# Moving the norm of the per-layer embedding e into the MLP, and rewriting the first stage, in a one-core decoder layer

## The chip, the core and the metric

The kernel runs on one core of a Trainium2 chip. The metric is the device time of one execution in microseconds (us). In the text PE is the matmul engine, DVE the vector engine, ACT the scalar engine, POOL the GpSimd engine, and SP the engine whose queue issues all the DMA transfers spoken of here. A line such as L1191 is a line of the kernel before; PEclk is the granted clock of PE as a share of full speed.

## The reference

One decoder layer over 2048 tokens of width 1024 in fp32. Two groups of token mixers share one input projection; their outputs go through one output projection; then comes an MLP with a squared ReLU, and last an embedding e, normed and gated, is added.

```python
hn = rms_norm(h, pre_mix_norm)
proj = hn @ w_in                    # q, k, v, z, a, b (DeltaNet); f, i, q, g (HGRN2)
g_dec = -exp(gdn_a_log) * softplus(a + gdn_dt_bias);  beta = sigmoid(b)
o_a = gated_head_norm(gated_delta_rule_chunked(l2norm(silu(conv(q))), l2norm(silu(conv(k))),
                                               silu(conv(v)), g_dec, beta), gdn_norm, z)
o_b = gated_head_norm(hgrn2_chunked(...), hgrn_norm, g)
h = h + rms_norm(concat(o_a, o_b) @ w_out, post_mix_norm)
y = square(relu(rms_norm(h, pre_mlp_norm) @ w_mlp_up)) @ w_mlp_down
h = h + rms_norm(y, post_mlp_norm)
e = rms_norm(p @ w_ple_proj, ple_norm)
h = h + e * sigmoid(h @ w_ple_gate)
```

## The kernel before

The tokens are worked on in four quarters q of 512, and a tile holds 128 channels by 512 tokens. Every fp32 product is made of three matmuls: each operand is split into a hi part (an ACT copy to fp32r) and a lo part, called its rest (a DVE subtract), and hi·hi, hi·lo and lo·hi are summed in PSUM. The function split does both steps (L169 on ACT, L170 on DVE). A weight passes from a raw tile to a split one in that way, and in the mixers also from there to a cache in DRAM.

The stages in order of PE's time:

- *Beginning.* e = p · w_ple_proj for q 0 and 1, 16 tiles (PE mme; ACT copies each to an SBUF tile, SP stores it to the DRAM tensor ed). The functions make, take and put issue the matmuls, the copy and the store of one tile. Between them x of q 0 is squared and normed (hl, nrm, ss, diag, ps_rsb), scaled (L458) and split into xt, and the projection ab (the rows for the decay and beta) goes into the bank mm_ab (L468).
- *Mixers.* 33 jobs for each quarter, each a block of 128 columns of w_in: 24 matmuls into a bank `mm` (L1191), and behind them the work of the heads as a list of steps. The banks come in turn from two PSUM pools, two banks of them in the pool pm. The quarter's first step is `decays`: it reads the bank mm_ab, makes softplus and sigmoid rows in the tile gb, scans them, and stores them (gd). gf_g is the broadcast load of gd for a head. `y_qg` and `y_kg` are q and k of DeltaNet after the convolution; kk_g are their products in a chunk, u_g and the solve follow, xn_g is its result in transposed form and psp_g the matmul that reads it.
- *Fill.* The same embedding for q 2 and 3 (embed_tile) among the last steps of the mixers.
- *Out-projection.* `mmo` (L1260), with w_out's blocks made ready by ready_out; behind it the residual yo and the sums acc_h and acc_o of its squares, and the norm of h.
- *MLP in two halves (q 0 and 1, then q 2 and 3).* Up (bank u, 16 blocks g) and down (bank d), each as seven products in place of eight of 2 x 2 blocks. up_weights loads the four parts `a` of a block's weights and makes wu; `hidden` stores the five combinations of the block's results that down reads. In half 0 `summed` squares and adds up the tiles of o for q 2 and 3. `residual` with the name "y" adds the normed y to h and stores it to h2d.
- *Gate.* `mmg`, and e times the gate.

The norm of e is a sum of squares over 8 tiles for each quarter. In the beginning squares(accs...) makes them from the SBUF copies for q 0 and 1, behind the last xt; in the fill from the banks for q 2 and 3. norm_steps turns each sum into a row ple_r[q], through DRAM for the transposition.

What sets the order: PE's instructions and SP's stand as the program writes them. In the beginning ACT and DVE do too. Elsewhere a scheduler orders ACT, DVE and POOL by due times, tc.issue_after ties an instruction behind another one, and high_priority ranks it above the rest. A clock ticks every 8 matmuls; at(...) and later(...) spread the steps of a generator over such ticks, a yield between two of them. An engine runs its instructions in order, and so does SP: a DMA that waits for its source or for its target buffer holds all that stand behind it.

Of the kernel before, what the change touches and what calls it, by code (L numbers as in the profile page):

```python
# [47 lines left out]
MLP_STEPS = (1, 5) + tuple(range(7, 25, 2))  # L48
# [37 lines left out]
def trunk(ctx, tc, x, xT, pT, vecs, w_in, w_ab, gdn_a_log, gdn_dt_bias, w_out, w_up, w_down,  # L86
# [56 lines left out]
    def bounds():  # L143

        V.tensor_scalar(ple_w, cols[:, R_PLE : R_PLE + KD], 0.5, None, ALU.mult)
        V.tensor_tensor(lb, lg, lg, ALU.subtract)
        S.activation(lb, lb, AF.Exp)
        V.reciprocal(lb1, lb)
        V.tensor_tensor(lb, lb, lb1, ALU.mult)
        V.tensor_tensor(lb, lb, lb, ALU.subtract)  # L150
        V.tensor_scalar(ha, lb, -0.5, 0.5, ALU.mult, ALU.add)
        V.tensor_scalar(hna, ha, -1.0, None, ALU.mult)
        V.tensor_tensor(hb, lb, ha, ALU.add)
        S.activation(nexpa, dec[:, 0:1], AF.Exp)
        V.tensor_scalar(nexpa, nexpa, -1.0, None, ALU.mult)
# [158 lines left out]
    def embed_tile(q, d, w, pt, accs, pool, bufs):  # L314
# [10 lines left out]
    x_r, xts, accs = {}, {0: []}, {0: None, 1: None}  # L325
# [26 lines left out]
    def ready_out(j):  # L352
# [42 lines left out]

    staged, split_w = {}, {}
    with ExitStack() as ectx:
        es = ectx.enter_context(tc.tile_pool(name="es", bufs=1))
        ET = mybir.EngineType
        with tc.manual_schedule(engines={ET.SP, ET.Activation, ET.DVE}):  # L400
            praw = [es.tile([P, 2, QT], F32, name=f"praw{q}") for q in range(2)]
            xraw = es.tile([P, KD, QT], F32, name="xraw")
            sqe = [es.tile([P, QT], F32, name=f"sqe{i}") for i in range(8)]
# [26 lines left out]
            last_x = []  # L430
# [22 lines left out]
            def square_e(i):  # L453
                q, d = todo[i]
                accs[q] = squares(accs[q], es16[i], d, f"e{q}", V, lambda: (sqe + sqx[2:])[i - 2 if i > 4 else i - 1])

# [3 lines left out]
            def ready_x0(k):  # L460
                t = ra.tile([P, 2, QT], F32R, tag="ring", name=f"xt0_{k}")
                last_x[:] = [S.activation(t[:, 0], xraw[:, k], AF.Copy).ins,
                             V.tensor_tensor(t[:, 1], xraw[:, k], t[:, 0], ALU.subtract).ins]
# [29 lines left out]
            take(5)  # L493
            make(8)
            make(9)
# [23 lines left out]
            make(12)  # L519
            for c in range(NC):  # L520
                PE.matmul(rsb[:, blk(c)], one, diag[:, c], start=True, stop=True)
            take(8)
            split_w[1] = staged.pop(1)()
            take(9)
            put(0, 1, 2)
            staged[2] = stage("0_0_0", w_in[0])
            put(3, 4, 5, 6)
# [3 lines left out]
            later_makes = {0: 13, 1: 14, 3: 15}  # L531
            gone = 10
            for k in range(KD):
# [7 lines left out]
                if k in later_makes:  # L541
                    make(later_makes[k])
                if k == 2:
                    put(7, 8, 9)
                    staged[3] = stage("8_0_0", w_in[8])
            while gone < 16:
                take(gone)
                gone += 1
            put(*range(10, 16))
        with tc.issue_after(last_x[0]), tc.issue_after(last_x[1]):  # L550
            bounds()
            for i in range(2 * KD):
                square_e(i)


    with mixers as mctx:
# [51 lines left out]
        def decays(ps, q):  # L608

            gb = mt(f"gb_{q}", "gb", 1, (36, QT))  # L610
            sp = m2.tile([4, QT], F32, tag="tmp", name=f"sp_{q}")
            se = m2.tile([4, QT], F32, tag="th", name=f"se_{q}")
            S.activation(sp, ps[0:4, :], AF.Identity, bias=dec[:, 1:2])
            V.memset(gb, 0.0)
            S.activation(gb[32:36, :], ps[32:36, :], AF.Tanh, scale=0.5)  # L615
            V.tensor_scalar(gb[32:36, :], gb[32:36, :], 0.5, 0.5, ALU.mult, ALU.add)
            V.scalar_tensor_tensor(se, sp, -1.0, sp, ALU.mult, ALU.max)
            S.activation(se, se, AF.Exp, scale=-1.0)
            S.activation(se, se, AF.Ln, bias=1.0)
            V.scalar_tensor_tensor(sp, sp, 0.0, se, ALU.max, ALU.add)  # L620
            V.tensor_scalar(sp, sp, nexpa, None, ALU.mult)
            tied = ExitStack()
            if q:
                yield
                tied.enter_context(tc.issue_after(turns[-1]))
            for c in range(NC):
                V.tensor_tensor_scan(gb[0:4, blk(c)], one[0:4, :], sp[:, blk(c)], 0.0, ALU.mult, ALU.add)
            tied.close()
            gd = dr.tile([4, QT], F32, name=f"gd{q}")
            decay[q] = [gd, None]  # L630
            yield
            nc.sync.dma_start(gd, gb[0:4, :])
# [537 lines left out]
        for q in range(2):  # L1170
            at(0, norm_steps(accs[q], 1.0 / D, EPS, f"e{q}", partial(ple_r.__setitem__, q)),
               [12 + 6 * q + i for i in (0, 2, 4, 5, 6)])
        with tc.manual_schedule(engines={mybir.EngineType.SP}):
            assert [w[0] for w in works[:4]] == ["ab0", "4_0_0", "0_0_0", "8_0_0"]
            for j, (name, key, src, q, h, then, g, b) in enumerate(works):
                split_work(j + 2)
                if j:
                    stage_work(j + 3)
                keep_work(j)
                ps = bank(f"mm_{name}") if j else ps_ab  # L1180
# [5 lines left out]
                for s in range(SPT):  # L1186
# [5 lines left out]
                    if s == SPT - 1 and h is None:  # L1192
                        at(clock[0], decays(ps, q) if q else urgent(decays(ps, q)), (0, 2.5, 3, 5) if q else (0, 2, 6))
# [9 lines left out]
            accs, store = {q: None for q in qs}, None  # L1203
# [20 lines left out]
            while clock[0] <= last or len(held) < 2 or 1 in ready:  # L1224
                if fill:
                    q, d = fill.pop(0)
                    new = embed_tile(q, d, ple[d // 4], pts[q], accs, m2, 2)
# [3 lines left out]
                    if d == KD - 1:  # L1231
                        at(clock[0], norm_steps(accs[q], 1.0 / D, EPS, f"e{q}", partial(ple_r.__setitem__, q)),
                           [1 + i for i in (0, 2, 4, 5, 6)])
# [84 lines left out]
    def residual(q, y_of, rsb, skip, gain, dst, name, sums=None, late=late):  # L1318
# [3 lines left out]
        total, put = None, None  # L1322
        for d in range(KD):
            yield
            if put:
                nc.sync.dma_start(*put)
# [4 lines left out]
            put = dst[d], y  # L1331
# [3 lines left out]
        yield  # L1335
        nc.sync.dma_start(*put)
# [25 lines left out]
    def summed(q):  # L1362

        total, y = None, late(yod[q][0], f"ys{q}_0")
        for d in range(KD):
            yield
            nxt = late(yod[q][d + 1], f"ys{q}_{d + 1}") if d + 1 < KD else None
            total = squares(total, y, d, f"o{q}")
            y = nxt
        yield  # L1370
        yield from rstd_steps(total, 1.0 / D, EPS, f"o{q}", row_of(o_r, q), po, wait=True)
# [245 lines left out]
    def hidden(half, g, c):  # L1617

        n = f"{half}_{g}"
        keep_hidden(half, g, "22", c["22"])  # L1620
# [9 lines left out]
        yield  # L1630
        for k, t in (("1", t1), ("3", c["12"]), ("2", t2), ("4", t4)):
# [207 lines left out]
    for half in range(2):  # L1839
        for g in range(NG):  # L1840
# [10 lines left out]
            if half == 0 and g in (1, 3):  # L1851
                later(summed((g + 3) // 2), list(range(2, 20, 2)) + [20, 30, 33])
# [112 lines left out]
```

## Time and profile before

| | us |
|---|---|
| runs, median (lowest to highest) | 2725.13 (2724.48 to 2728.61) |
| profiled execution | 2726.73 |
| its span | 2724.9 |
| PE busy in the span | 2663.4 (98%) |
| DVE busy | 2046.8 (75%) |
| ACT busy | 1473.0 (54%) |

The profiled execution is one run of its own, with a granted clock of 0.995 on the mean. Busy shares are means over the whole span; the stages differ. PE's matmuls of 128x512 follow each other every 0.24 us in an undisturbed stretch (24 in 5.71 us), so a gap of a few us between two of them is a wait that the views name.

### The profile page before, as it was taken

What the parts mean: (1) busy time and instruction counts of PE and PEld (TensorE: products, weight loads), DVE (VectorE), ACT (ScalarE), POOL (GpSimd) and SP (SyncE); (2) the same over time, 40 slices, a digit from 0 to 9 for tenths busy, and PEclk for the clock granted to TensorE, in tenths of its full rate; (3) what the DMA queues carried; (4) which work ended last, traced back from release to release, by engine and by line L of the source; (5) the groups of instructions that cost most, each with busy time, mean ns of one, the idle gap of its engine ahead of it and who ended that gap; (6) DMA issues with size and microseconds to landing.
All of it is one profiled execution on the core that took longest, in us unless ns stands there. A gap on an engine that the chain in (4) does not pass through costs nothing. (4 is left out here: it accounts for less than half of the span.)

```text
span 2724.9 us, 38478 instructions
## 1 busy us (share of the span) xinstructions
PE 2663.4 (98%) x12761; PEld 2219.2 (81%) x12761; DVE 2046.8 (75%) x4243; ACT 1473.0 (54%) x2951; POOL 107.6 (4%) x118
## 2 busy tenths in 40 slices
PE   7899999999999999999999999999999999999999
PEld 5788788888888888778887788887888888887887
DVE  7788877787788777678779977858787765567775
ACT  6666555455546445676565556545555445465431
POOL 0000000000000000000000000001000000001000
PEclk9999999999999999999999999999999999999999
DMA  6867777666666665888456666657454356677663
GB/s 222 271 232 239 234 252 239 219 220 241 240 209 220 208 211 180 255 295 282 141 189 213 241 211 223 225 192 249 161 187 166 137 187 196 195 255 243 207 219 124
DMA packets 271223, 587.93 MB, mean 216 GB/s; under 512 B 55706, under 2 KB 60280, under 8 KB 253616
## 3 DMA queue, kind: packets, MB, share of 16 engines
q1 hardware_dynamic: 271024, 585.48, 64.2%
q8 instruction: 101, 1.65, 0.2%
q14 instruction: 98, 0.80, 0.1%
HBM read 421.58 MB, written 163.77 MB: 215 GB/s over the span
## 5 line engine op out<-in xcount | busy, mean ns | idle before, releaser
L1191 PE MATMUL mm<-xt,w 128*128 128x512 f32 x3072 | 785.3, 402 | 11.1 <-ACT gb L615 7.7
L1191 PEld LDWEIGHTS mm<-xt,w 128*128 128x128 f32 x3072 | 557.3, 189 | 116.2 <-ACT gb L615 8.1
L1260 PE MATMUL d<-db,da 128*128 128x512 f32 x2688 | 614.2, 391 | 3.9 <-DVE db L223 2.1
L1260 PE MATMUL u<-t,wu 128*128 128x512 f32 x2604 | 595.1, 391 | 4.8 <-ACT wu L169 3.7
L1260 PEld LDWEIGHTS d<-db,da 128*128 128x128 f32 x2688 | 505.5, 188 | 111.9 <-DVE db L223 4.5
L1260 PEld LDWEIGHTS u<-t,wu 128*128 128x128 f32 x2604 | 489.6, 188 | 109.3 <-ACT wu L169 4.8
L223 DVE TENSOR_TENSOR db<-db 128x512 fp32r<-128x512 f32 x224 | 160.8, 718 | 71.4 <-ACT db L222 70.0
L1645 DVE TENSOR_TENSOR u<-u,u 128x512 f32<-128x512 f32 x224 | 151.1, 685 | 59.8 <-PE u L1260 58.8
L222 ACT ACTIVATE db<-db 128x512 fp32r<-128x512 f32 x224 | 140.9, 629 | 81.3 <-DMA db<-hid 78.9
L1260 PE MATMUL mmg<-h2T,wg 128*128 128x512 f32 (+1 forms) x792 | 174.8, 383 | 0.0
L1260 PEld LDWEIGHTS mmg<-h2T,wg 128*128 128x128 f32 x792 | 145.7, 188 | 28.9
L1686 ACT ACTIVATE u<-u 128x512 f32<-128x512 f32 x128 | 80.8, 631 | 163.1 <-DVE u L1645 162.6
L1260 PE MATMUL mmo<-mixT,w_out 128*128 128x512 f32 x720 | 165.9, 392 | 2.5 <-DVE w_out L170 2.5
L1260 PEld LDWEIGHTS mmo<-mixT,w_out 128*128 128x128 f32 x720 | 136.3, 189 | 31.2 <-DVE w_out L170 2.9
L170 DVE TENSOR_TENSOR da<-da 128x512 fp32r<-128x512 f32 x128 | 94.1, 735 | 88.6 <-ACT da L169 88.2
L169 ACT ACTIVATE da<-da 128x512 fp32r<-128x512 f32 x128 | 80.5, 629 | 135.7 <-DMA da<-sumd 108.3
L169 ACT ACTIVATE wu<-a 128x512 fp32r<-128x512 f32 x124 | 74.0, 622 | 48.4 <-DMA a<-in_w_up_dram 45.7
L828 DVE TENSOR_TENSOR pr_g<-xs_g,sys_g 128x16 f32<-128x16 f32 (+14 forms) x240 | 94.2, 392 | 5.3
L233 POOL TENSOR_TENSOR acc_y<-acc_y,sq_y 128x512 f32<-128x512 f32 x28 | 38.6, 1378 | 1371.0 <-ACT sq_y L232 1371.0
L170 DVE TENSOR_TENSOR wu<-a,wu 128x512 fp32r<-128x512 f32 x124 | 85.2, 689 | 3.4 <-ACT wu L169 3.4
L1687 ACT ACTIVATE u<-u 128x512 f32<-128x512 f32 x128 | 80.6, 630 | 3.4
L170 DVE TENSOR_TENSOR da<-dr,da 128x512 fp32r<-128x512 f32 x96 | 66.4, 691 | 17.7 <-ACT da L169 15.4
(397 smaller groups left out, 3817.2 us busy)
## 6 DMA issues: line engine op xcount, KB each, us to landing
w<-cache_in SPq DMA_DIRECT2D x96, 1024.0 KB
db<-hid SPq DMA_DIRECT2D x224, 256.0 KB
cache_in<-w SPq DMA_DIRECT2D x32, 1024.0 KB
hid<-u SPq DMA_DIRECT2D x128, 256.0 KB
da<-sumd SPq DMA_DIRECT2D x128, 256.0 KB
a<-in_w_up_dram SPq DMA_DIRECT2D x124, 256.0 KB
hid<-ht SPq DMA_DIRECT2D x96, 256.0 KB
dr<-in_w_down_dram SPq DMA_DIRECT2D x96, 256.0 KB
```

The lines of the kernel that those rows point to most:

```text
L169: S.activation(t[:, 0], raw, AF.Copy)
L170: eng.tensor_tensor(t[:, 1], raw, t[:, 0], ALU.subtract)
L222: S.activation(t[:, 0], plain(t), AF.Copy)
L223: V.tensor_tensor(t[:, 1], plain(t), t[:, 0], ALU.subtract)
L233: eng.tensor_tensor(acc, acc, sq, ALU.add)
L828: V.tensor_tensor(pr[:, :, :, 0:i], xs[:, None, :, 0:i].broadcast_to([P, 2, GC, i]), sys[:, 0:i, i : i + 2].rearrange("p j two -> p two j" ...
L1191: PE.matmul(ps, *terms[i], start=i == 0, stop=i == nt - 1)
L1260: PE.matmul(ps, a, b, start=start, stop=stop)
L1645: V.tensor_tensor(c[new], c[old], ps, ALU.add)
L1686: S.activation(c[k], c[k], AF.Relu)
L1687: S.activation(c[k], c[k], AF.Square)
```

## The change

It has five parts.

1. *Norm of e.* The squares, the adds and the steps of its norm leave the beginning and the fill. In half 1 of the MLP `summed`, with source, name and target as arguments, loads the eight tiles of e of one quarter from ed, squares and adds them, and makes the row; one quarter each at the blocks g = 3, 6, 9 and 12 of the up projection.
2. *Beginning.* The order of makes, takes and puts is new; the rests of w_ab and of w_4_0_0 come earlier; w_0_0_0 is split in the loop over k; the load of 8_0_0 comes last. The rows of the decay for q 0 (decay_rows, the old body of decays) are made right behind ab, before the mixers begin. bounds() is left to the scheduler.
3. *Bank.* Job 2 takes its bank from the pool pp.
4. *w_out.* For the first blocks the rest is issued with high priority.
5. *Stores.* `hidden` issues the store of "22" one step later, beside the other four, except for the block (1, 0). `residual` with the name "y" stores a tile two steps behind its add, not one.

The core of the diff:

```diff
-MLP_STEPS = (1, 5) + tuple(range(7, 25, 2))
+MLP_STEPS = (1, 5) + tuple(range(7, 27, 2))
...
-        accs[q] = squares(accs[q], ps, d, f"e{q}")            # embed_tile
...
         if q < RAW:                                            # ready_out
-            split(w, V, raw)
+            S.activation(w[:, 0], raw, AF.Copy)
+            with tc.high_priority():
+                V.tensor_tensor(w[:, 1], raw, w[:, 0], ALU.subtract)
...
+    def decay_rows(ps, gb, sp, se, tied=ExitStack):
+        S.activation(sp, ps[0:4, :], AF.Identity, bias=dec[:, 1:2])
+        V.memset(gb[0:32, :], 0.0)
+        S.activation(gb[32:36, :], ps[32:36, :], AF.Tanh, scale=0.5)
...
             square_x(6)                                        # beginning
...
-            make(10)
+            make(9)
             w = split_w[0] = wp.tile([P, 2, KD, P], F32R, tag="whl", name="w_ab0")
             S.activation(w[:, 0], raw, AF.Copy)
+            V.tensor_tensor(w[:, 1], raw, w[:, 0], ALU.subtract)
...
-            V.tensor_tensor(w[:, 1], raw, w[:, 0], ALU.subtract)
+            make(10)
             make(11)
+            split_w[1] = staged.pop(1)()
+            take(8)
+            take(9)
             diag = sqx[1].rearrange("p (c j) -> p c j", c=NC)
...
-            split_w[1] = staged.pop(1)()
...
                 ready_x0(k)
-                if gone in sums:
-                    take(gone)
-                    gone += 1
+                if k in (0, 2, 4, 6):
+                    take(12 + k // 2)
+                elif k == 5:
+                    split_w[2] = wp.tile([P, 2, KD, P], F32R, tag="whl", name="w_0_0_0")
+                    S.activation(split_w[2][:, 0], staged[2], AF.Copy)
                 ab(k)
...
-                    staged[3] = stage("8_0_0", w_in[8])
...
+            put(*range(13, 16))
+            keep("ab", split_w[0])
+            staged[3] = stage("8_0_0", w_in[8])
+            for _ in decay_rows(ps_ab, first_gb, rest[:, 0], rest[:, 1]):
+                pass
-            bounds()
-            for i in range(2 * KD):
-                square_e(i)
+        bounds()
...
-                ps = bank(f"mm_{name}") if j else ps_ab
+                ps = bank(f"mm_{name}", pp if j == 2 else None) if j else ps_ab
...
-        total, put = None, None                                # residual
+        total, puts, lag = None, [], 2 if name == "y" else 1
...
-            if put:
-                nc.sync.dma_start(*put)
+            if len(puts) == lag:
+                nc.sync.dma_start(*puts.pop(0))
             if d + 1 < KD:
                 nxt, ynxt = late(skip(d + 1), f"x{name}{q}_{d + 1}"), y_of(d + 1)
...
-        keep_hidden(half, g, "22", c["22"])                    # hidden
+        if not STRASSEN_DOWN or (half, g) == (1, 0):
+            keep_hidden(half, g, "22", c["22"])
...
         yield
+        if (half, g) != (1, 0):
+            keep_hidden(half, g, "22", c["22"])
         for k, t in (("1", t1), ("3", c["12"]), ("2", t2), ("4", t4)):
...
+            if half == 1 and g in (3, 6, 9, 12):
+                q = g // 3 - 1
+                later(summed(q, ed[q], "e", ple_r), list(range(2, 26, 3)) + [26, 28, 32, 36])
```

How the order moves, at three places. A row gives the line, the operation, out<-in by name and number, and the shape; both kernels are listed apart, since lines and buffer numbers differ between them.

First ACT where the mixers begin. Before (sqx are squares of e here, sp and gb_657 the reading of the bank mm_ab):

```order
L232 ACTIVATE sqx_256<-e_272 128x512
L232 ACTIVATE sqx_257<-e_273 128x512
L232 ACTIVATE sqx_258<-e_274 128x512
L169 ACTIVATE w_0_0_652<-raw_0_0_468 128x1024
L169 ACTIVATE w_0_0_674<-raw_0_0_518 128x1024
L169 ACTIVATE hl_e_868<-acc_e_582 128x512
L613 ACTIVATE sp_658<-mm_ab_476,dec 4x512
L665 ACTIVATE acc_kg_0_707<-mm_0_0_681,cols 128x512
L666 ACTIVATE hist<-mm_0_0_681 128x3
L615 ACTIVATE gb_657<-mm_ab_476 4x512
```

After (xt_6 and xt_7 are the last tiles of the loop, sp_570 and gb_569 the reading of mm_ab):

```order
L456 ACTIVATE e_266<-mme_7_520 128x512
L167 ACTIVATE xt_7_555<-xraw 128x512
L397 ACTIVATE sp_570<-mm_ab_472,dec 4x512
L399 ACTIVATE gb_569<-mm_ab_472 4x512
L402 ACTIVATE sp_570<-sp_570 4x512
L404 ACT_TABLE_LOAD
L404 ACTIVATE sp_570<-sp_570 4x512
L675 ACTIVATE acc_kg_0_666<-mm_0_0_639,cols 128x512
L167 ACTIVATE w_0_0_632<-raw_0_0_567 128x1024
L676 ACTIVATE hist<-mm_0_0_639 128x3
```

The reading of mm_ab stood behind the squares of e, two weight copies and hl_e, with acc_kg of the next bank between its two halves; now it follows the last xt at once, and acc_kg comes behind it.

Second ACT around q of the first DeltaNet head (acc_qg is the start of its convolution, jk the sums of squares of k, cd, tail, e and kt read gf_g). Before:

```order
L665 ACTIVATE acc_qg_0_761<-mm_0_0_722,cols 128x512
L666 ACTIVATE hist<-mm_0_0_722 128x3
L678 ACTIVATE y_qg_0_768<-acc_qg_0_761 128x512
L765 ACTIVATE jk_g_0_0_816,ssk_g_0_805<-t_kg_0_810 128x128
L765 ACTIVATE jk_g_0_1_818,ssk_g_0_805<-t_kg_0_810 128x128
L765 ACTIVATE jk_g_0_2_820,ssk_g_0_805<-t_kg_0_810 128x128
L765 ACTIVATE jk_g_0_3_822,ssk_g_0_805<-t_kg_0_810 128x128
L169 ACTIVATE w_0_0_769<-raw_0_0_718 128x1024
L744 ACT_TABLE_LOAD
L744 ACTIVATE cd_g_0_785<-gf_g_0_731 128x4
L746 ACTIVATE tail_g_0_786<-tail_g_0_786 128x4
L750 ACTIVATE e_g_0_790<-e_g_0_790,gcol_758 128x128 x4
```

After:

```order
L167 ACTIVATE w_0_0_728<-raw_0_0_677 128x1024
L754 ACT_TABLE_LOAD
L754 ACTIVATE cd_g_0_744<-gf_g_0_690 128x4
L756 ACTIVATE tail_g_0_745<-tail_g_0_745 128x4
L760 ACTIVATE e_g_0_749<-e_g_0_749,gcol_717 128x128 x4
L761 ACTIVATE gf_g_0_690<-gf_g_0_690 128x512
L775 ACTIVATE jk_g_0_3_781,ssk_g_0_764<-t_kg_0_769 128x128
L777 ACTIVATE kt_g_0_774<-t_kg_0_769,tail_g_0_745 128x128 x4
L688 ACT_TABLE_LOAD
L688 ACTIVATE y_qg_0_727<-acc_qg_0_720 128x512
```

y_qg stood right behind the convolution and ahead of the work on gf_g; now it stands behind all of that and behind a table load of its own.

Third DVE in the out-projection (sq_h and sqo are squares of yo and of mmo; w_out_12909 is the block whose subtract starts at 1205.98 in the profile). Before:

```order
L1329 SCALAR_TENSOR_TENSOR yo_6_12594<-yo_6_12594,cols,r_o_12712 128x512
L233 TENSOR_TENSOR acc_h_12756<-acc_h_12756,sq_h_5_12857 128x512
L1330 TENSOR_TENSOR yo_6_12594<-yo_6_12594,xa_6_12766 128x512
L1329 SCALAR_TENSOR_TENSOR yo_7_12633<-yo_7_12633,cols,r_o_12712 128x512
L223 TENSOR_TENSOR mixT_6_12892<-mixT_6_12892 128x512
L1330 TENSOR_TENSOR yo_7_12633<-yo_7_12633,xa_6_12766 128x512
L233 TENSOR_TENSOR acc_h_12756<-acc_h_12756,sq_h_6_12875 128x512
L233 TENSOR_TENSOR acc_o_12679<-acc_o_12679,sqo_4_12906 128x512
L170 TENSOR_TENSOR w_out_12909<-raw_out_12851,w_out_12909 128x1024
L233 TENSOR_TENSOR acc_h_12756<-acc_h_12756,sq_h_7_12889 128x512
```

After:

```order
L231 TENSOR_TENSOR acc_o_12532<-acc_o_12532,sqo_3_12698 128x512
L231 TENSOR_TENSOR acc_h_12609<-acc_h_12609,sq_h_3_12667 128x512
L1336 TENSOR_TENSOR yo_4_12363<-yo_4_12363,xa_4_12593 128x512
L1335 SCALAR_TENSOR_TENSOR yo_5_12404<-yo_5_12404,cols,r_o_12565 128x512
L361 TENSOR_TENSOR w_out_12762<-raw_out_12704,w_out_12762 128x1024
L231 TENSOR_TENSOR acc_h_12609<-acc_h_12609,sq_h_4_12685 128x512
L1336 TENSOR_TENSOR yo_5_12404<-yo_5_12404,xa_4_12593 128x512
L1335 SCALAR_TENSOR_TENSOR yo_6_12447<-yo_6_12447,cols,r_o_12565 128x512
L1335 SCALAR_TENSOR_TENSOR yo_7_12486<-yo_7_12486,cols,r_o_12565 128x512
L231 TENSOR_TENSOR acc_h_12609<-acc_h_12609,sq_h_5_12710 128x512
```

Before, w_out_12909 stood among the sums of sq_h_6, sq_h_7 and sqo_4. The same block after, w_out_12762, stands ahead of the sum of sq_h_4 and of the last three steps on yo.

More of the change, by code (lines that the diff above doesn't have):

```diff
@@ L461, in ready_x0 @@
                 t = ra.tile([P, 2, QT], F32R, tag="ring", name=f"xt0_{k}")
-                last_x[:] = [S.activation(t[:, 0], xraw[:, k], AF.Copy).ins,
-                             V.tensor_tensor(t[:, 1], xraw[:, k], t[:, 0], ALU.subtract).ins]
+                split(t, V, xraw[:, k])
                 xts[0].append(t)
@@ L608, in decays @@
         def decays(ps, q):
[L610 to L622, printed above, removed]
-            if q:
-                yield
[L625 to L632, printed above, removed]
+            if q:
+                gb = mt(f"gb_{q}", "gb", 1, (36, QT))
+                rows = decay_rows(ps, gb, m2.tile([4, QT], F32, tag="tmp", name=f"sp_{q}"),
+                                  m2.tile([4, QT], F32, tag="th", name=f"se_{q}"),
+                                  lambda: tc.issue_after(turns[-1]))
+                for _ in range(3):
+                    next(rows)
+                yield
+                next(rows, None)
+                gd = dr.tile([4, QT], F32, name=f"gd{q}")
+                decay[q] = [gd, None]
+                yield
+                nc.sync.dma_start(gd, gb[0:4, :])
+            else:
+                gb, gd = first_gb, dr.tile([4, QT], F32, name="gd0")
+                decay[q] = [gd, None]
+                nc.sync.dma_start(gd, gb[0:4, :])
             yield
@@ L1334, in residual @@
             xk, y = nxt, ynxt
-        yield
-        nc.sync.dma_start(*put)
+        while puts:
+            yield
+            nc.sync.dma_start(*puts.pop(0))
         return total
```

91 lines of the change are left out of this document (46 added, 45 removed).

## The prediction

> **What bounds the kernel.** I read the page's engine shares first, then the waits of PE, then stretches of the span, then the timeline around each wait that the change touches. First the page:
>
> ```profile
> span 2724.9 us, 38478 instructions
> PE 2663.4 (98%) x12761; PEld 2219.2 (81%) x12761; DVE 2046.8 (75%) x4243; ACT 1473.0 (54%) x2951; POOL 107.6 (4%) x118
> ```
>
> PE is the bound. The change takes no matmul away: the eight that sum the squares of e for the norm are issued elsewhere. So it can only win what PE idles, 61.5 us (2724.9 less 2663.4), and what a cold clock costs behind an idle stretch. The waits of PE, as line waited for, total, times, longest:
>
> ```profile
> PE mm L1191 <- ACT gb L615: 7.7, 1, 7.7
> ...
> PE psp_g L852 <- DVE xn_g L847: 6.0, 2, 4.3
> ...
> PE u L1260 <- ACT wu L169: 3.7, 2, 2.8
> PE mmo L1260 <- DVE w_out L170: 2.5, 1, 2.5
> ...
> PE mm_ab L468 <- ACT xt L462: 1.9, 1, 1.9
> ...
> PE d L1260 <- ACT db L222: 1.7, 1, 1.7
> PE mm L1191 <- ACT zt_zg L704: 1.7, 1, 1.7
> PE nrm_h L1292 <- DVE hl_h L170: 1.2, 2, 0.6
> ...
> PE mme L196 <- ACT sq_e L232: 0.9, 1, 0.9
> PE mme L196 <- ACT acc_e L229: 0.9, 1, 0.9
> ```
>
> The waits are short ones in known places, and the edits aim at gb, xt, sq_e, acc_e, w_out, wu and db. Stretches of the span (length, busy time of each engine, granted clock, DMA share, GB/s):
>
> ```profile
> 30.00:40.00 10.00, 8.29 (x28) 6.49 (x29) 8.69 (x15) 6.03 (x11) 0.00 (x0) 0.83 1.00 360
> 50.00:60.00 10.00, 2.84 (x7) 2.27 (x8) 9.79 (x15) 8.01 (x13) 3.02 (x15) 0.67 0.47 156
> 1060.00:1120.00 60.00, 54.79 (x305) 45.35 (x304) 49.52 (x116) 42.27 (x92) 3.13 (x3) 1.00 0.55 171
> 1200.00:1210.00 10.00, 7.51 (x29) 5.78 (x28) 8.82 (x14) 7.37 (x13) 0.00 (x0) 0.86 0.61 219
> 1323.00:1383.00 60.00, 59.10 (x260) 48.41 (x259) 53.14 (x87) 41.53 (x73) 0.00 (x0) 1.00 0.63 207
> 1950.00:2240.00 290.00, 290.00 (x1281) 240.29 (x1281) 221.12 (x351) 148.03 (x246) 0.00 (x0) 1.00 0.49 169
> ```
>
> The reader sees three tight places (50 to 60, the fill at 1060 to 1120, 1200 to 1210) and one with no slack to win, the up projection of half 1 (1950 to 2240), where PE never stops.
>
> **The change, part by part.** *The beginning up to the ab projection.* DVE sets the pace of the loop that scales x and splits it into xt:
>
> ```profile
> 30.02 1.40 DVE L458 SCALAR_TENSOR_TENSOR xraw<-xraw,cols,ps_rsb 128x512 f32<-128x512 f32 x2
> 39.14 0.69 DVE L463 TENSOR_TENSOR xt<-xraw,xt 128x512 fp32r<-128x512 f32 x1 [1.27 <-ACT xt L462]
> 41.88 1.29 DVE L463 TENSOR_TENSOR xt<-xraw,xt 128x512 fp32r<-128x512 f32 x2 [1.39 <-ACT xt L462]
> ```
>
> Its two waits for ACT are 1.27 + 1.39 = 2.66 us; there ACT held a copy of e behind a matmul of PE. The new loop takes a copy of e only at k = 0, 2, 4, 6, from banks filled earlier. The subtract for w_4_0_0 (128x1024) stood between diag and the first scale and now stands ahead of diag, while ss is still being formed: another 1.2 us. Together 3.9; I take -3.5, and as ends -1.3 (one wait stays) and -4.5 (with the clock of 0.83 between 30 and 40 mended).
>
> *The wait for gb.* The third bank user waits until mm_ab's bank has been read, and that reading stands behind the squares of e:
>
> ```profile
> 47.67 3.22 ACT L232 ACTIVATE sqx<-e 128x512 f32<-128x512 f32 x6
> 49.78 3.30 DVE L233 TENSOR_TENSOR acc_e<-acc_e,sqx 128x512 f32<-128x512 f32 x5
> 56.00 0.48 DVE L614 MEMSET gb<- 36x512 f32 x1
> 56.52 0.59 ACT L615 ACTIVATE gb<-mm_ab 4x512 f32<-4x512 f32 x1 [0.32 <-DVE gb L614]
> 57.16 7.19 PE L1191 MATMUL mm<-xt,w 128*128 128x512 f32 x24 [7.65 <-ACT gb L615]
> 68.78 5.71 PE L1191 MATMUL mm<-xt,w 128*128 128x512 f32 x24
> ```
>
> With the squares and adds gone, gb read right after ab, and job 2's bank taken from the other pool, nothing of this is left: -7.65, and -1.48 for the 24 matmuls that ran cold (7.19 against 5.71): -9.1. Ends: -9.3, and -5 if job 3's weights, whose load now goes out last of the beginning, are the next to be late.
>
> *What is late next: y_qg.* The order of ACT now puts the table load, cd, tail, e, gf, kt and a second table load ahead of y_qg, which before stood ahead of them. The rows of before:
>
> ```profile
> 64.42 0.32 SPq L734 DMA_DIRECT2D gf_g<-gd  x1
> ...
> 68.12 0.63 ACT L678 ACTIVATE y_qg<-acc_qg 128x512 f32<-128x512 f32 x1 [2.98 <-DVE acc_qg L670]
> ...
> 71.42 1.28 ACT L744 ACT_TABLE_LOAD   x1
> 72.71 0.21 ACT L744 ACTIVATE cd_g<-gf_g 128x4 f32<-128x4 f32 x1
> ...
> 74.62 1.10 ACT L767 ACTIVATE kt_g<-t_kg,tail_g 128x128 f32<-128x128 f32 x4
> ...
> 74.33 0.38 PE L788 MATMUL kk_g<-y_kg 128*128 128x128 f32 x2
> ```
>
> The first use of the loaded gf, from the view of its tile:
>
> ```profile
> L745 DVE TENSOR_TENSOR tail_g<-gf_g,gcol x16: 155/157/171, 72.1 to 999.4; 128x4 f32<-128x4 f32 x16
> ```
>
> The first job ended at 57.16 - 7.65 = 49.5, so the mixers began at 49.5 - 5.7 = 43.8; after, at 40.3, with job 2 from 46.0. kk stood 74.33 - 57.16 = 17.2 us behind job 2's start, 15.7 without the cold 1.5, so kk is due at 61.7, and t_kg (done at 68.78, 5.55 ahead of kk) at 56.15. ACT finished kt at 75.72, 6.9 us behind t_kg: after, at 63.1. One more table load (1.28) and y_qg (0.63) end at 65.0, so kk waits 3.3 us; gf's load (72.1 - 64.42 = 7.7 from issue to use) is due at about 57, before ACT asks for it. I add 1 for a colder clock behind it: +4.3. Ends: 0 (ACT runs ahead, as it has 16 squares less behind it) and +7.
>
> The Trainium skill ("ScalarE: Activation LUTs", What ACT_TABLE_LOAD costs) counts 1.28 us for a table load and 1.38 more for a drain; by it the two loads would delay y_qg by 2.8 more, kk would wait 6, and the sum would be 2.8 smaller. The row at 72.71, 1.29 behind the load's start, leaves no room for a drain behind the load, so I go by 1.28. The same skill ("TensorE: Matmul & The Clock Gate", Part 1) lets the clock drop only after an idle window of some 3.4 us, by which a wait of 3.3 adds nothing; but here the clock was 0.86 between 1200 and 1210 around a wait of 2.5, so the 1 us stays.
>
> *The waits behind.* zt (1.7) stood behind a table load that now comes earlier on ACT: -1.7, ends 0 and -1.7. psp_g's 4.3 waits for xn, the end of the triangular solve that starts at kk. Its chain shifts with kk, and the rest of the mixers' order is unchanged: 0, with ends -4.3 and +3 (kk's delay passed on).
>
> *The fill.* 16 squares and 14 adds of e leave ACT and DVE. PE was idle 60 - 54.79 = 5.2 us in 1060 to 1120, of which 0.9 + 0.9 were on sq_e and acc_e; the other waits there are on ACT, which has some 10 us less to do. I take -3; ends -1.8 and -5.2.
>
> *w_out's rests.* The late subtract and the copy ahead of it:
>
> ```profile
> 1202.53 1.06 ACT L169 ACTIVATE w_out<-raw_out 128x1024 fp32r<-128x1024 f32 x1
> ...
> 1205.98 1.22 DVE L170 TENSOR_TENSOR w_out<-raw_out,w_out 128x1024 fp32r<-128x1024 f32 x1
> ```
>
> The hi part was done at 1203.6, and DVE did scales and sums of yo first. In the new order nine of these operations stand behind the subtract, so it can start 2.4 us earlier and the wait of 2.5 goes, and with it up to 1.4 of a clock of 0.86. What is late next is acc_h and so nrm_h (0.6 before). -3; ends -3.9 and -1.
>
> *The stores in the MLP.*
>
> ```profile
> 1454.07 2.00 SPq L1567 DMA_DIRECT2D a<-in_w_up_dram  x4
> 2475.77 0.32 SPq L1326 DMA_DIRECT2D h2d<-y  x1
> ```
>
> The loads of a at 1454 stood behind stores of hidden tiles; the longest wait for wu (2.8) follows them, but ACT's own queue, where sq_h waited for yp, had its part. -1; ends 0 and -4.4. The tile "22" is held longer in its ring of 16, which could delay loads of a instead. For y, the lag of two does not help: the store at 2475.77 blocked SP until y's add was done, and the load of the next skip tile needs that same add, since its tag has two buffers. So SP stops at the load in place of the store, and db's 1.7 stays: 0; ends 0 and -3.
>
> *The norm of e in half 1.* Each quarter brings 8 loads of 256 KB, 8 squares, 7 adds, a split, two matmuls, and the rstd with two table loads. The nearest rows are those of the same routine on o in half 0:
>
> ```profile
> L232 ACT ACTIVATE sq_o<-ys x14: 615/632/635, 1339.6 to 1400.5; 128x512 f32<-128x512 f32 x14
> L233 DVE TENSOR_TENSOR acc_o<-acc_o,sq_o x14: 685/687/693, 1340.7 to 1401.5; 128x512 f32<-128x512 f32 x14
> ```
>
> Four quarters at 12 operations of 0.69 give DVE 33 us; at 12 of 0.63 and 2 loads of 1.28, ACT gets 40. In 1950 to 2240 DVE goes from 221 to 254 of 290 (88%), ACT from 148 to 188 (65%). In 1323 to 1383 DVE was at 53.14 of 60 (89%) with the same sums, and PE ran 59.10. So it lies beside PE's work: +0.5 for the four waits of nrm_e on its split, ends 0 and +6.
>
> **The sum:** -3.5 - 9.1 + 4.3 - 1.7 + 0 - 3 - 3 - 1 + 0 + 0.5 = -16.5. The profiled execution took 2726.73, so 2710.2; it lay 1.6 above the median of the runs (2725.13), so 2708.6. A change under 0.2% (5.4 us) can't be told from none here.
>
> **Rivals.**
> - *The solve keeps its time.* kk waits 7, and xn comes 3 later than now against PE: -16.5 + 2.7 + 3 = -10.8, so 2714. For it: xn's wait was 4.3 already. Against: that wait was shared with other work of DVE.
> - *All of it works.* kk waits 0, the fill gives 5.2, w_out 3.9, wu 4.4: -27, so 2698. Against: each needs a queue with no next thing late.
> - *A wait replaces gb's.* Job 3's weights or y_qg hold PE for as long as gb did, and kk waits 7: -16.5 + 9.1 + 2.7 = -4.7, so 2720.4, no change that can be told. For it: the first 40 us have a DMA share of 1.00, and job 3's load is last. Against: from 40 on the queue is freer, and 11 us are left.
> - *Slower: e's tiles hold up half 1.* The 32 loads of e go through two buffers on SP, in one queue with the loads of a and the hidden stores. When a step's square or add is late, SP stops and the next a behind it is late. It turns the result once a step costs PE over 16.5/32 = 0.5 us; at the 0.9 of an mme wait it is +29, so 2737. For it: half 1 has no idle PE to hide it. Against: the step comes every third tick, and half 0 did the same every second one.
>
> **Chances.** The forecast 0.62 (own range 2702 to 2716), the solve 0.15, all of it 0.10, a wait in gb's place 0.09, e in half 1 0.04. Faster by over 0.2%: 0.62 + 0.15 + 0.10 = 0.87; no change 0.09; slower 0.04. The range reaches to "all of it" and most of the way to the replaced wait: 2698 to 2719.
>
> **What would show it.** In the profile of the changed kernel the wait for gb is gone and the clock in 50 to 60 is near 1.0; PE waits about 3 us at kk for y_qg; psp_g still waits about 4; mmo no longer waits for w_out; mme has no wait on e's sums; d's wait for db near the end is still there; and 1950 to 2240, shifted by some 15 us, has PE without a gap with DVE near 88%. The prediction is wrong if PE shows gaps in that stretch, if another wait over 5 us stands in the first 60 us, or if psp_g's wait grows by as much as gb's shrank.

## The result, and the profile after

The changed kernel took 2712.88 us (median of four runs, 2710.64 to 2715.24), the kernel before 2725.38 on the same chip (the mean of the two middle runs, of which the table ahead gives the lower). The ratio of the runs is 0.9945 (95% interval 0.9932 to 0.9959): 12.5 us or 0.55% faster, against 16.5 forecast. The profiled execution took 2714.24. Its page begins:

```profile
span 2712.5 us, 38506 instructions
PE 2658.5 (98%) x12761; PEld 2213.8 (82%) x12761; DVE 2054.6 (76%) x4255; ACT 1485.0 (55%) x2967; POOL 101.8 (4%) x114
```

The matmuls are as many as before, and PE idles 54 us in place of 61.5. Its waits after (line waited for, total, times, longest):

```profile
PE nrm_h L1297 <- ACT hl_h L167: 8.1, 2, 7.5
...
PE mme L194 <- ACT e L316: 3.2, 3, 2.6
PE kk_g L799 <- ACT y_qg L688: 2.7, 1, 2.7
PE psp_g L862 <- DVE xn_g L857: 2.7, 2, 1.7
...
PE nrm_h L1298 <- DVE hl_h L168: 1.6, 2, 1.2
...
PE u L1266 <- ACT wu L167: 0.8, 1, 0.8
PE mm L1200 <- ACT zt_zg L714: 0.7, 1, 0.7
PE d L1266 <- ACT db L220: 0.7, 2, 0.4
```

The waits for gb and for w_out are gone, those for wu and db are small. Three are new: kk for y_qg, mme for the copies of e, and, the largest, nrm_h for hl_h. (nrm_h is the matmul that adds acc_h up over the channels, hl_h the split of acc_h that it reads; db is the split tile that a matmul of down reads.) Stretches after, answering to those of before (length, busy time, clock, DMA share, GB/s):

```profile
50.00:60.00 10.00, 10.00 (x49) 8.03 (x48) 7.46 (x15) 6.00 (x14) 0.00 (x0) 1.00 0.95 296
60.00:70.00 10.00, 7.05 (x38) 5.62 (x37) 5.35 (x13) 8.31 (x21) 1.01 (x1) 1.00 0.67 243
1050.00:1110.00 60.00, 54.50 (x302) 45.92 (x302) 39.42 (x93) 34.01 (x71) 2.12 (x2) 1.00 0.58 188
1225.00:1246.00 21.00, 14.01 (x62) 11.26 (x60) 21.00 (x32) 10.76 (x18) 0.00 (x0) 0.91 0.78 269
1940.00:2230.00 290.00, 290.00 (x1282) 240.11 (x1281) 244.54 (x395) 181.23 (x303) 0.00 (x0) 1.00 0.59 200
```

50 to 60 is full at full clock. In the fill (1050 to 1110) ACT and DVE are 8 to 10 us lighter than before, but PE idles as much. In 1225 to 1246 DVE has no free moment and PE loses 7. Half 1 (1940 to 2230) carries e's norm without a gap.

Where the time went is read best by following one matmul through both traces. Five of them, in the timeline of before:

```profile
43.90 5.60 PE L1191 MATMUL mm<-xt,w 128*128 128x512 f32 x24
...
132.36 0.60 PE L852 MATMUL psx_g<-part,xt_g 128*128 128x128 f32 x4
...
1253.60 0.50 PE L1291 MATMUL nrm_h<-hl_h,ones 128*128 128x512 f32 x1 [0.52 <-ACT hl_h L169]
...
1304.08 19.22 PE L1260 MATMUL u<-t,w_u 128*128 128x512 f32 x84
...
1461.86 8.52 PE L1260 MATMUL u<-t,wu 128*128 128x512 f32 x28 [2.85 <-ACT wu L169]
```

and the first four in that of after:

```profile
41.93 11.06 PE L1200 MATMUL mm<-xt,w 128*128 128x512 f32 x48
...
116.19 0.68 PE L862 MATMUL psx_g<-part,xt_g 128*128 128x128 f32 x4
...
1246.52 0.79 PE L1297 MATMUL nrm_h<-hl_h,ones 128*128 128x512 f32 x1 [7.51 <-ACT hl_h L167]
...
1299.25 19.20 PE L1266 MATMUL u<-t,w_u 128*128 128x512 f32 x84
```

The same for more matmuls (negative is earlier):

| matmul | before | after | lead |
|---|---|---|---|
| first of the mixers | 43.90 | 41.93 | -2.0 |
| first kk with y_qg | 74.55 | 66.09 | -8.5 |
| first psx_g | 132.36 | 116.19 | -16.2 |
| first mmo | 1119.2 | 1103.8 | -15.4 |
| second nrm_h of the out-projection | 1253.60 | 1246.52 | -7.1 |
| first u of half 0 | 1304.08 | 1299.25 | -4.8 |
| the u that waited for wu | 1461.86 | 1453.95 | -7.9 |
| first d of half 0 | 1620.06 | 1607.18 | -12.9 |
| end of the last matmul | 2720.1 | 2707.1 | -13.0 |

So 16 us are won by 130, 10.6 are lost between the first mmo and the first u, and 8 to 9 are won again in the up projection of half 0: just ahead of the u that waited for wu the lead is still -4.9. Between 130 and 1100 the lead wanders between -18.7 and -13.5.

The loss in the out-projection has three places. At the last heads' norm the waits of PE are 1.3 and 0.3 us, but the matmuls behind them run cold (0.56 in 1119 to 1122), and 3.8 us are lost:

```profile
1118.15 0.50 PE L267 MATMUL nrm_g<-hl_g,ones 128*128 128x512 f32 x1 [1.32 <-ACT hl_g L167]
```

At w_out 4.3 us are won. At the first nrm_h 2.3 are lost, and at the second 9.2, of which 2.2 come behind the wait of 7.5, in cold matmuls again (0.63 in 1245 to 1255).

### The profile page after: what moved, and what is told of

The parts are those of the page before. It is cut to its first block, busy times and chain, and to the rows that moved or that the text cites. A ratio compares the mean times of both kernels' runs of the same rounds, so it can differ in the third digit from the quotient of the medians.

```text
span 2712.5 us, 38506 instructions
## 1 busy us (share of the span) xinstructions
PE 2658.5 (98%) x12761; PEld 2213.8 (82%) x12761; DVE 2054.6 (76%) x4255; ACT 1485.0 (55%) x2967; POOL 101.8 (4%) x114
## 4 chain that ended last, share of the span: by engine, by line
PE 50%; DVE 4%; DMA 3%; issue 3%; ACT 2%; POOL 1%; SPq 0%; POOLq 0%; DVEq 0%; ACTq 0%
PE u L1266 22%; PE d L1266 19%; PE mmg L1266 6%; PE mmo L1266 2%; DMA da<-sumd 1%; DMA mixT<-mixd 1%; POOL acc_y L231 1%; DVE w_out L361 0%; DVE yo L1336 0%; DMA raw_out<-in_w_out_dram 0%; DVE yo L1335 0%; DVE acc_h L231 0%; ACT sq_y L230 0%; DMA dr<-in_w_down_dram 0%; DMA h2d<-y 0%
## 5 line engine op out<-in xcount | busy, mean ns | idle before, releaser
L168 DVE TENSOR_TENSOR da<-dr,da 128x512 fp32r<-128x512 f32 x96 | 66.3, 691 | 17.6 <-ACT da L167 15.4
```

Source lines behind the costliest of these rows:

```text
L168: eng.tensor_tensor(t[:, 1], raw, t[:, 0], ALU.subtract)
```

## The experiments

All edits start from the changed kernel unless the text says before. Two profiles of the very same kernel already differ by some us, so in each case the place in the trace decides and the time stands beside it.

**The changed kernel again**, with no edit:

> The changed kernel unchanged, as a measure of the others on this chip: 2710 to 2715, with the same waits in the fill (copies of e, about 3), at nrm_h (7 to 8) and at kk (2.7); the mixers between 130 and 1060 wander by a few us.

2712.89 us (2708.41 to 2716.24), ratio 0.9938 (0.9918 to 0.9958). Against the first profile the lead of PE's matmuls moved by -2.6 to 0 between 270 and 810, and by -3.9 at the end; most of that came between 1118 and 1202, where nrm_g and the first nrm_h waited 2 us less and lost less to a cold clock. So a step of up to 4 us there says nothing of an edit. The other waits named were there again (kk 2.7, mme 2.8, second nrm_h 7.5); the last is 7.3 to 7.5 in all seven profiles whose edit lies elsewhere. What follows reads steps of the lead, not totals.

**The priority of w_out undone:**

```diff
-            with tc.high_priority():
-                V.tensor_tensor(w[:, 1], raw, w[:, 0], ALU.subtract)
+            V.tensor_tensor(w[:, 1], raw, w[:, 0], ALU.subtract)
```

> The changed kernel, with the rest of w_out scheduled as before (no high priority). Theory A, the price moved: in the changed kernel the subtracts put ahead hold back the sums acc_h, so that the second nrm_h waits 7.5 us; without the priority that wait falls under 1.5 us, mmo waits some 2.5 us for w_out again, and, since PE then reaches the MLP 5 to 7 us earlier while the engines beside it do not, the wait for wu near 1450 comes back in part (1 to 4 us). Time 2705 to 2711. Rival B, the wait of nrm_h is not from the priority but from the whole stage arriving earlier: it stays over 5 us, mmo waits for w_out as well, and the time is 2713 to 2718. Rival C, the terms are independent: nrm_h's wait goes and nothing comes back behind it: about 2713 - 11 + 4 = 2704 to 2706.

2708.07 us (2703.97 to 2712.32), 0.9932 (0.9916 to 0.9949). Its waits in the out-projection:

```profile
PE mmo L1265 <- DVE w_out L360: 4.8, 2, 4.0
PE nrm_h L1296 <- ACT hl_h L167: 3.6, 1, 3.6
```

In the trace PE lost 6.1 us against the changed kernel near 1200 and got 6.6 back at the two nrm_h. The priority moved a wait from w_out to nrm_h and was worth nothing by itself, give or take half a us. None of the three theories was right as a whole: nrm_h kept 3.6, so half of its 7.5 is not the priority's; and the wait for wu did not come back.

**The store of 22 back where it was:**

```diff
-        if not STRASSEN_DOWN or (half, g) == (1, 0):
+        if True:
             keep_hidden(half, g, "22", c["22"])
...
-        if (half, g) != (1, 0):
+        if False:
             keep_hidden(half, g, "22", c["22"])
```

> The changed kernel, with the store of the combination 22 of hidden issued at once, as before. Theory A: the wait for wu near 1461 of the kernel before was taken up by PE coming later out of the out-projection, not by this store; undoing it brings no wait over 1 us for wu, and the time stays at 2712 to 2714. Rival C: the store ahead of the loads of a made that wait; with it back, PE waits 2 to 3 us for wu near 1450, with a colder clock, and the time is 2716 to 2719.

2717.17 us (2714.07 to 2719.43), 0.9963 (0.9950 to 0.9975). The waits of PE between 1430 and 1570:

```profile
PE u L1266 <- ACT wu L167: 2.8, 1, 2.8
PE u L1266 <- DVE wu L168: 0.9, 1, 0.9
```

From 1450 to 1640 PE lost some 9 us against the changed kernel. Rival C was right about the edit, its place and its price, and theory A, that PE's own lateness had swallowed the wait for wu, falls.

How the store does it is another matter. The longest wait of SP just ahead of the late wu is 5.3 us, at the store (L1618) of a tile that ACT has yet to square; but the changed kernel, where PE waits for nothing, has a wait of 5.4 us at the same store. The store of 22 itself stopped SP for 2.3 to 3.4 us in three of the blocks ahead, with the loads of a behind it. More was lost on ACT, 40 us earlier: with the store early, the scheduler puts the first step of the row r_o ahead of two squares of u, and with the store late behind them. ACT then stands at that step until acc_o is ready; first this run, then the changed kernel:

```profile
1411.23 0.63 ACT L1302 ACTIVATE r_o<-acc_o 128x512 f32<-128x512 f32 x1 [8.68 <-DVE acc_o L1301]
```

```profile
1414.98 0.63 ACT L1302 ACTIVATE r_o<-acc_o 128x512 f32<-128x512 f32 x1 [2.48 <-DVE acc_o L1301]
```

SP's longest wait for the squares was 12.6 us here and 7.2 in the changed kernel, and from there on ACT was later against PE than in the changed kernel, by 5 to 11 us, and by 7 at the wait for wu. The other profiles agree: in the kernel before, and in the same without e's norm, both with the store early, ACT stood 8.1 and 7.2 us at r_o and PE waited 2.8 and 2.6 for wu; in all eleven profiles with the store late ACT stood 2.5 and PE did not wait. No run moved the store and kept ACT's order, so how the 8 to 9 us divide between the two is not shown.

**The store of 22 moved in the kernel before**, the same edit the other way, alone:

> The kernel before with one edit, the store of 22 one step later. Theory J, the store alone makes the waits for wu near 1461 and 1563, because SP stops at it until its tile is squared, with the loads of yp and a behind it: these waits go, with the cold clock, and half 0's up projection is 6 to 8 us shorter; 5 to 8 us below the kernel before. Rival: in the kernel before, ACT's wait for yp holds wu, and at least 2 us of the wait stay; 0 to 3 us below.

2722.33 us (2714.81 to 2728.00) against 2730.65 of the kernel before on that chip, 0.9971 (0.9959 to 0.9983), 8 us. Between 1440 and 1580 PE has no wait left that the view lists. In this profile PE was 8.9 us behind the kernel before at 1451, although no engine's order differs up to 1300; by 1629 it was 0.3 behind, so 8.6 us were won. Theory J holds for the edit, which is worth nearly as much as the removed wait for gb. Its reason, SP's stop alone, is not shown: ACT's wait at r_o fell here too, from 8.1 to 2.5.

**The lag of y's stores undone:**

```diff
-        total, puts, lag = None, [], 2 if name == "y" else 1
+        total, puts, lag = None, [], 1
```

> The changed kernel, with the lag of one for the stores of y, as before. Theory A: SP stops at the load of the next skip tile for the same add at which it stopped for the store, so nothing moves: no wait over 1 us for db behind 2450 and 2712 to 2714. Rival: the lag was what removed the wait of 1.7 us for db; it comes back near 2470 with a cold clock, and the time is 2715 to 2717.

2710.10 us (2706.75 to 2711.99), 0.9938 (0.9924 to 0.9953). The lead did not step by 1 us anywhere behind 1140, and between 2400 and 2545 PE waited for db 0.2 (on ACT) and 0.9 (on DVE). The lag does nothing; that db's wait of 1.7 for ACT went has another cause. It was gone in the kernel before with the store of 22 moved (1.5 on DVE in its place) and in the kernel before without e's norm (0.9 in all) as well. It may belong to the one profile of the kernel before; this was not followed further.

**Half 1 without e's norm** (rows of o's norm in its place):

```diff
-                later(summed(q, ed[q], "e", ple_r), list(range(2, 26, 3)) + [26, 28, 32, 36])
+                ple_r[q] = o_r[2 + q % 2]
```

> The changed kernel without the norm of e: no load, square, add or matmul for it in half 1, and the gate takes the rows of o's norm in its place (the output lacks the right norm of e). Theory A: that work lies beside PE's in half 1, so only the eight matmuls of nrm_e go, 1.8 us: 2710 to 2712, and PE has no gap in 1940 to 2230 with or without it. Rival: the sums delay something later (the loads for down, or y's chain), which goes with them: 2704 to 2709.

2706.06 us (2702.82 to 2709.17), 0.9925 (0.9910 to 0.9940). The stretch of half 1's up projection without it:

```profile
1930.00:2220.00 290.00, 290.00 (x1281) 240.23 (x1280) 220.69 (x350) 146.60 (x247) 0.00 (x0) 1.00 0.49 168
```

DVE falls from 244.5 to 220.7 and ACT from 181 to 147; PE is full with it and without it. Behind 1930 PE's lead grew by some 2.8 us, of which the eight matmuls are 1.8. So e's norm is hidden there within about a us.

**The kernel before without e's norm**, in the beginning and in the fill, with nothing in its place; its diff is the removal of square_e, of the squares in embed_tile and of both norm_steps:

> The kernel before without the norm of e: no squares, adds, matmuls or row steps for it in the beginning and the fill, and nothing in their place (the gate takes rows of o's norm). Theory D, the squares alone made the wait for gb: ACT reads mm_ab's bank near 44 to 46, the wait for gb (7.7) and the cold clock behind it are gone without the rewritten beginning, and by the matmul psp_g near 127 PE is 9 to 13 us ahead of the kernel before. Rival E, the rest of the old order (the weight copies, the bank's turn, hl) holds the bank as well: the wait for gb stays over 3 us. Time by D 2710 to 2716, by E 2717 to 2722. In both, the waits for w_out (2.5) and wu (2.8) stay.

2725.73 us (2723.66 to 2729.59) against 2729.64, 0.9984 (0.9972 to 0.9995). Its waits:

```profile
PE nrm_h L1282 <- ACT hl_h L169: 3.6, 1, 3.6
PE mmo L1251 <- DVE w_out L170: 3.6, 2, 3.0
PE u L1251 <- ACT wu L169: 3.4, 2, 2.6
...
PE mme L196 <- ACT e L318: 3.0, 2, 2.6
...
PE kk_g L786 <- ACT y_qg L675: 2.7, 1, 2.7
```

Theory D holds for the cause: without e's norm the wait for gb is gone in the old order too, and at psp_g PE is 11 us ahead (12 just behind it). But the end is only about 1 us earlier in the trace, and 3.9 by the medians. The lead fell by some 4 us over the mixers (no more than they wander), by 8 between the first mmo and the matmuls just behind the out-projection's second nrm_h, and by 1.5 more near 1450. The time of my expectation was wrong because I thought a lead once won would stay.

**y_qg first on ACT:**

```diff
+                elif name == "qg0_0":
+                    with tc.high_priority():
+                        S.activation(y, acc, AF.Silu)
```

> The changed kernel, with the first y_qg on ACT ahead of the table load and of the work on gf (one instruction with high priority). Theory F, the beginning is bound by DMA and by the solve behind kk: kk's wait of 2.7 goes, but psp_g, which waits 1.0 for xn, then waits 2 to 4, so that behind 125 PE is less than 1.5 us ahead of the changed kernel. Rival: the 2.7 us stay won at 125. Time by F 2711 to 2714, by the rival 2709 to 2711; the place in the trace decides, since the mixers wander by a few us.

2712.45 us (2707.82 to 2715.24), 0.9935 (0.9911 to 0.9961). kk waits no more, and PE is 2.9 us further ahead there; its waits between 30 and 130:

```profile
PE mm L1203 <- ACT zt_zg L717: 1.9, 1, 1.9
PE psx_g L865 <- POOL rk_g L163: 1.0, 1, 1.0
PE psp_g L865 <- DVE acc_qg L680: 0.5, 1, 0.5
```

By 127 all of it is given back, as theory F said, though at zt and psx and not at xn.

**Four tiles for the copies of e in the fill:**

```diff
-        e = pool.tile([P, QT], F32, tag="ld", name=f"e{q}_{d}", bufs=bufs)
+        e = pool.tile([P, QT], F32, tag="ld" if d % 2 else "tmp", name=f"e{q}_{d}")
```

> The changed kernel, with four SBUF tiles in place of two for the copies of e in the fill (every second one in the ring of another tag). Theory G: in the fill the copy of e waits for the store of the tile two before it, and PE for the copy (3.2 us, longest 2.6); with four tiles these waits fall under 0.8 us in all and PE leaves the fill 2 to 4 us earlier than in the changed kernel, counted from 1060. Rival: SP, which stops at a store until its copy is made, is the next thing late, and the fill keeps its time within 1 us. Time by G 2709 to 2712, by the rival 2712 to 2714.

2705.17 us (2703.89 to 2705.86), 0.9909 (0.9880 to 0.9937), the lowest median of all, though its interval touches that of the changed kernel (0.9932 to 0.9959). The fill, and the out-projection's waits:

```profile
1045.00:1110.00 65.00, 62.44 (x348) 52.24 (x348) 44.37 (x105) 37.16 (x78) 3.12 (x3) 1.00 0.64 197
```

```profile
PE nrm_h L1297 <- ACT hl_h L167: 4.2, 2, 3.5
...
PE mmo L1266 <- ACT w_out L359: 0.9, 1, 0.9
PE mmo L1266 <- DVE w_out L361: 0.7, 1, 0.7
```

No mme waits for a copy of e. What held the fill in the changed kernel is seen on SP (its timeline):

```profile
1084.49 5.97 SPq L317 DMA_DIRECT2D ed<-e  x2
```

With two tiles, the second of these stores waits for its copy, the copy for the landing of a store made earlier, and all of SP's queue behind them waits too, the loads and stores of the heads' last norms among them. Theory G was right on the fill: PE gained 3.7 us there against the changed kernel. At w_out 2 us were lost, and 4.1 came at the second nrm_h; but the scheduler ordered DVE and ACT otherwise in the out-projection of this run, so those two are not the tiles' alone.

**be held behind r_o:**

```diff
+            with tc.issue_after(made["o1"]):      # the last DVE step of r_o, quarter 1
                 V.scalar_tensor_tensor(first_b[kk], first_b[kk], col(R_PREMLP + kk), h1_r[0], ...)
```

> The changed kernel, with the scaling of h for the MLP's first operands (be on DVE, t behind it) held back until r_o of quarter 1 is made. Theory H: the wait of 7.5 us at the second nrm_h is DVE's: five be and five t stand between nrm_o and r_o and among the sums acc_h; with them behind, hl_h comes 3 to 6 us earlier against PE, the wait falls to 2 to 4 us, and the time to 2707 to 2711, if the MLP's first matmuls do not wait for t in their place. Rival: the chain is held by the loads of mixT and the table loads on ACT, and the wait stays at 6 to 7.5 us; or it falls and u's first matmul waits as much (2712 to 2715).

2711.20 us (2708.45 to 2714.55), 0.9932 (0.9907 to 0.9957). The largest wait of the out-projection is now

```profile
PE nrm_h L1298 <- ACT hl_h L167: 4.3, 2, 4.1
```

and PE gained 3.4 us at that matmul; the MLP's first matmuls did not wait in its place. Theory H holds for 3.4 of the 7.5 us: be and t stood ahead of r_o and among the sums. In this profile the mixers ran some 3 us later than in the first one, so the time shows less than the place.

**Both repairs together** (four tiles, be behind r_o):

> The changed kernel with both repairs, four tiles for the copies of e in the fill and be held behind r_o. If the two waits are separate, the fill gains 3 to 4 us and the nrm_h wait falls to 0 to 2 us: 2700 to 2704, below both kernels. If the out-projection's chain has one bound for both (the end of the mixers' heads and the loads of mixT), only one of them counts: 2704 to 2708.

2705.83 us (2703.90 to 2707.93), 0.9910 (0.9896 to 0.9925). The fill gained as with four tiles alone, nrm_h kept 4.9 and w_out 1.8: the two do not add up. What holds the stage once both are in (the last heads' norms, the loads of mixT, DVE's total or the order that the scheduler chose) was not taken apart.

**Job 2's bank back in pm** (None in place of pp):

> The changed kernel with job 2's bank from the pool pm again. Theory: the bank plays no part any more, since sp and gb read mm_ab right behind the last xt, two jobs' time before the third bank user needs it: no wait of mm on gb, 41 to 55 without a gap, 2710 to 2715. Rival: the bank was needed, and mm waits 1 to 4 us near 47 or 52.

2712.70 us (2710.91 to 2718.03), 0.9939 (0.9922 to 0.9955). The stretch with the three first jobs:

```profile
41.50:55.00 13.50, 13.50 (x62) 10.94 (x61) 11.06 (x22) 8.72 (x13) 3.42 (x15) 1.00 0.95 306
```

PE is full: the bank's pool plays no part.

## Why the prediction was right, and where its terms were off

The sign, the size (2708.6 forecast, 2712.9 measured) and most places were right. But four terms missed by some -5 (psp_g), +2 (fill), +14 (out-projection) and -8 us (store of 22); that they nearly cancel is luck. Two of the signs named failed as well: psp_g was to wait about 4 still, and db 1.7.

- *Beginning, -3.5:* -2.0 in the first profile, where PE's waits for ACT at mm_ab fell from 1.9 to 0.4 and the first mixers' matmul moved from 43.90 to 41.93. In the eleven profiles with this beginning it is -2.0 to -4.2, the middle one -3.5, as forecast.
- *gb, -9.1:* -9.4; the wait of 7.65 and the cold clock are gone. The run without e's norm shows that this norm alone had made it; neither the bank nor the rewriting was needed.
- *y_qg next, +4.3:* +2.7, at the place named. By the forecast the wait itself was 3.3; what I added for a cold clock did not come (1.00 in 60 to 70). The second table load began at 64.12, right behind kt, and y_qg at 65.41. Here the Trainium skill's idle window of some 3.4 us ("TensorE: Matmul & The Clock Gate", Part 1) agreed with the trace, though not at the shorter waits at w_out and nrm_g (last section); its extra drain ("ScalarE: Activation LUTs", What ACT_TABLE_LOAD costs), by which kk would have waited an estimated 6, does not show. Behind it zt (-1.7) gave -1.4.
- *psp_g, 0:* the step that failed most in the beginning. Its wait fell from 4.3 to 1.0, with the cold clock behind it. I let the solve move exactly with PE. But kk's new wait held PE, and DVE's weight split ahead of xn, which waits for the cache's store, was not held with it: it came at 111.28, 0.8 ahead of the time at which PE was ready, and before at 125.86, 2.2 behind it. A lead of 16 us by 130 in place of 10 is mostly this (4.6 us from just ahead of psp_g to psx_g). It is read from the rows; no run took it apart.
- *Fill, -3:* about -1 by the first mmo, half of it two matmuls of nrm_e that left. I took the ACT and DVE work off and named no next thing late; it was the round trip of the stores through two tiles, as the four tiles show.
- *w_out, -3:* the largest miss: -4.3 at w_out, +11.5 at the two nrm_h, and +3.8 at nrm_g, which had no term (+1.1 there in the second profile). "What is late next is acc_h and so nrm_h" was named, but priced from a wait of 0.6. My reading is that DVE, at 18.87 of 20 us there before, could not follow a PE that came 15 us earlier. That is argued and holds only in part: in the changed kernel DVE was busy 15.97 of 20 us from 1205 on, and full only from 1225. Undoing the priority, holding be back, and four tiles each took 3.4 to 4 us off the wait of 7.5; what holds the rest stays open.
- *Store of 22, -1 (0 to -4.4):* -8.6, outside my ends. I looked only at the rows next to the wait, and read ACT's sq_h, which waited for yp, as a second cause. But sq_h waits for yp as long after (3.61 us) as before (3.84). The lateness came from 40 us earlier, where ACT stood at r_o for 8.1 us before and 2.5 after, in another order of the scheduler, which I had not looked for.
- *Lag of y, 0; e's norm in half 1, +0.5:* the lag does nothing and e's norm is hidden, as forecast and shown by the runs without them (DVE came to 84% there, not 88%). But "db's 1.7 stays" failed: it went, with 1.6 us of lead, and not by the lag.

Of the rivals, none came as written. What "the solve keeps its time" has in common with the result is that a lead is given back later, though in the out-projection and not at the solve.

## What to carry to other kernels

A lead won on the bounding engine stays only if the stages behind it can come earlier too. Look for the next stage in which another engine is nearly full (here DVE, 18.87 of 20 us), and price the lead there as a wait: taking e's norm out won 11 us by 130 and kept 1 in the trace and 4 by the medians. Read the waits of the DMA issuing queue as well as those of the engines: a ring of two tiles under a store cost 3.7 us in the fill. And where a scheduler orders the engines, compare their orders before naming a cause: one store moved by one step was worth 8 to 9 us, and with it a wait on ACT moved that no edit had touched. A wait that stands in the fast kernel too (SP's 5.3 and 5.4 us) does not explain the difference.

## What was not expected of the hardware

A wait of 2.7 us at kk left the clock at 1.00, while before, one of 2.5 us between 1200 and 1210 came with 0.86, and after, the 1.3 and 0.3 us at nrm_g came with 0.56 in the three us behind them:

```profile
1119.00:1122.00 3.00, 3.00 (x8) 2.40 (x9) 0.44 (x1) 2.43 (x5) 0.00 (x0) 0.56 0.78 249
```

The length of a wait of this size does not by itself say whether the clock falls. And the matmuls of one and the same program wander over the mixers from one execution to the next: at 1060 five profiles, of the changed kernel and of its variants, whose programs do not differ up to there, lie up to 5.4 us apart, and two of the kernel before 7.2 us at the first mmo. Four runs spread over 2 to 8 us. Without the places in the traces, half of the verdicts above could not have been given.
